# Activations or weights as the stationary operand: gates, outputs and feed-forward of one encoder block moved from "features by tokens" to "tokens by features"

## The chip, the cores and the metric

One core of a Trainium2 chip runs the whole block once. The metric is the device time of that run in microseconds (us). The kernel before took 1521.12 us (median of 3 runs, 1521.03 to 1523.44).

## What is computed

One layer on 256 tokens of width 2048, all in float32 (D = 2048, 16 heads of 128, feed-forward width 5632):

```python
h = rmsnorm(x, g_mix)
q_sb, k_sb, v_sb, q_ca, k_ca, v_ca, gate_sb, gate_ca = split(h @ w_in)     # 2048 x 10240
y_sb = stick_breaking_attention(q_sb, k_sb, v_sb)                           # 8 heads
y_ca = chunked_relpos_attention(q_ca, k_ca, v_ca, rel_bias)                 # 8 heads
merged = sigmoid(gate_sb) * (y_sb @ w_sb_out) + sigmoid(gate_ca) * (y_ca @ w_ca_out)
x = x + merged @ w_mix_out
g, u = split(rmsnorm(x, g_ffn) @ w_ffn_in)                                  # 2048 x 2*5632
x = x + (silu(g) * u) @ w_ffn_out
x = x + sigmoid(rmsnorm(x, g_ple) @ w_ple_gate) * (p @ w_ple_in)
out = rmsnorm(x, g_final)
```

## The kernel before

**Products.** Every large product is a list of *pieces*. A piece is one load of 512 KB of weights into a buffer `raw` (L147, queue of SP). ScalarE rounds it to `hi` (L176), VectorE takes the rest `lo = raw - hi` (L177), and TensorE multiplies (`products`, L188). The activations are kept in tables of the same two parts, features on the partitions: `T1`, `T2`, `T3`, each [128, 16, 2, 256] (feature tile, hi or lo, token). An exact enough float32 product is hi·hi + hi·lo + lo·hi.

There are two kinds of group (L129):

- `feat`: the **weights** are stationary. 256 output columns a group, four feature tiles a piece. For one feature tile and 128 output columns there is one matmul of 512 columns (`hi` with both parts of the table side by side, L201) and one of 256 (`lo` with the table's hi part, L203). The output is features by tokens, in two halves of a PSUM bank that `halves` (L231) adds up with one ScalarE copy and one VectorE add.
- `row`: the **activations** are stationary. 512 output columns a group, two feature tiles a piece, and for each feature tile and 128 tokens three matmuls of 512 columns (L184, L185, L186). The output is tokens by features, complete in one bank.

Before, the values of both attentions, `p @ w_ple_in` and the last product with `w_ple_gate` are `row`; all else is `feat`. So the residual is held as `xT`, features by tokens; `put_split` (L239) and `put_split_gain` (L243) make the next table straight from a group's output, and only the last stage turns `xT` back (`x2_chunk`, L668: 32 transposes).

**Norms.** The sums of squares are partial sums on GpSimd over the feature tiles (L93 to L97), finished by a matmul with ones (`nps`, L105); a further matmul (`rps`, L115) spreads the result over all partitions for `feat` groups (`rbc`).

**Order.** `flush` (L220) walks the pieces. Loads run five pieces ahead and the splitting two; a queue `tasks` gives attention steps and the like, run between pieces. A scheduler then sets each engine's final order from its own estimate of the times, so PE's order at the start is not that of the code.

**Stages, in order:** start (transposes of x, values of the first heads, `w_ple_in`), queries, keys, values and attention, gates, output products (`w_sb_out`, `w_ca_out`), `w_mix_out`, feed-forward in three blocks (16, 16 and 12 feature tiles wide), `w_ple_gate` with the final norm.

Of the kernel before, what the change touches and what calls it, by code (L numbers as in the profile page):

```python
# [16 lines left out]
P = 128  # L17
# [23 lines left out]
def block_kernel(ctx: ExitStack, tc: tile.TileContext, x, p, w_in, w_sb_out, w_ca_out, w_mix_out,  # L41
# [6 lines left out]

    nc = tc.nc
# [22 lines left out]
    const("fill", [P, 344])  # L72
# [18 lines left out]
    sqs = const("sqs", [P, 2, S])  # L91

    def square_sum(kt, sq):  # L93
        if kt == 0:
            nc.gpsimd.tensor_copy(sqs, sq)
        else:
            nc.gpsimd.tensor_tensor(sqs, sqs, sq, ALU.add)  # L97

    def norm(n):

        both = sqs[:, 0, :]
# [118 lines left out]
    def flush(every=1):  # L220

        while state["at"] < len(pieces):
# [16 lines left out]
    def put_split(dst, kt, src):  # L239
        nc.scalar.copy(dst[:, kt, 0, :], src)  # L240
        nc.vector.tensor_tensor(dst[:, kt, 1, :], src, dst.bitcast(F32)[:, kt, 0, :], ALU.subtract)

    def put_split_gain(dst, kt, src, gain):  # L243
        g = gT[:, gain + kt : gain + kt + 1]
        nc.scalar.activation(dst[:, kt, 0, :], src, AF.Identity, scale=g)
        nc.vector.scalar_tensor_tensor(dst[:, kt, 1, :], src, g, dst.bitcast(F32)[:, kt, 0, :],  # L246
                                       ALU.mult, ALU.subtract)
# [8 lines left out]
    xt = sp.tile([P, NT, D], F32, tag="xt", name="xt")  # L256
# [12 lines left out]
    def x_tiles(kt, ps):  # L269

        n = ps.shape[1]
        for k in range(n):
            for t in range(NT):
                nc.tensor.transpose(ps[:, k, t * P : (t + 1) * P], xt[:, t, (kt + k) * P : (kt + k + 1) * P], ident)
# [10 lines left out]
        nc.scalar.copy(xT[:, kt : kt + n, :], ps)  # L285

    def x_pair(kt):
# [5 lines left out]
        xk = xT[:, kt : kt + 2, :]  # L293
        sq = sp.tile([P, 2, S], F32, tag="sq", name="sq", bufs=2)
        nc.gpsimd.tensor_tensor(sq, xk, xk, ALU.mult)  # L295
        square_sum(kt, sq)
# [86 lines left out]
    gates = ap.tile([P, 2, KD, S], F32, tag="gates", name="gates", bufs=1)  # L383
# [172 lines left out]
    def gate_post(m, j):  # L556
        def post(ps):
            for f in range(2):
                sm = halves(ps[f], mp)
                nc.vector.tensor_tensor(gates[:, m, 2 * j + f, :], sm, rbc, ALU.mult)  # L560
        return post

    for j in range(8):
        for m in range(2):
            group("feat", w2, 6 * W + m * D + j * FB, range(KD), T1, gate_post(m, j), needs=hneed)
    flush(4)

    def out_post(m, j):
        def post(ps):
            gt = gates[:, m, 2 * j : 2 * j + 2, :]  # L570
            nc.scalar.activation(gt, gt, AF.Sigmoid)
            for f in range(2):
                kt = 2 * j + f
                sm = halves(ps[f], mp)
                nc.vector.tensor_tensor(gates[:, m, kt, :], sm, gates[:, m, kt, :], ALU.mult)
            if m == 1:
                for kt in (2 * j, 2 * j + 1):
                    mg = gates[:, 0, kt, :]
                    nc.gpsimd.tensor_tensor(mg, mg, gates[:, 1, kt, :], ALU.add)  # L579
                    put_split(T1, kt, mg)  # L580
        return post

    for j in range(8):
# [3 lines left out]
    flush(4)  # L587
    while tasks:
        run_task()
# [6 lines left out]
    x2 = lp.tile([P, NT, D], F32, tag="x2", name="x2")  # L596
    gf = lp.tile([P, D], F32, tag="gf", name="gf")
    dma_x.dma_start(gf, g_final.rearrange("(o d) -> o d", o=1).to_broadcast((P, D)))
    def norm_task(n):
        norm(n)  # L600
        if n == "ffn":
            tasks.append((None, lambda: broadcast_rstd(n, lp)))

    def residual_post(j, dst, gain, norm_of):

        def post(ps):
            for f in range(2):
                kt = 2 * j + f
                xk = xT[:, kt, :]
                nc.vector.tensor_tensor(xk, ps[f][:, :S], xk, ALU.add)  # L610
                nc.vector.tensor_tensor(xk, ps[f][:, S:], xk, ALU.add)  # L611
                if dst is not None:
                    put_split_gain(dst, kt, xk, gain)
            if dst is not None:
                sq = lp.tile([P, 2, S], F32, tag="tg", name="sq", bufs=2)
                nc.scalar.activation(sq, xT[:, 2 * j : 2 * j + 2, :], AF.Square)  # L616
                square_sum(2 * j, sq)
                if j == 7:
                    tasks.append((None, lambda: None))
                    tasks.append((None, lambda: norm_task(norm_of)))  # L620
        return post

    for j in range(8):
        group("feat", w_mix_out[0], j * FB, range(KD), T1, residual_post(j, T3, 16, "ffn"))
# [4 lines left out]
    def g_post(j):  # L629
        def post(ps):  # L630
            tg = lp.tile([P, 2, S], F32, tag="tg", name="tg", bufs=2)
            sg = lp.tile([P, 2, S], F32, tag="sg", name="sg", bufs=2)
            for f in range(2):
                sm = halves(ps[f], lp)
                nc.vector.tensor_tensor(tg[:, f, :], sm, rbc, ALU.mult)
            nc.scalar.activation(sg, tg, AF.Sigmoid)  # L636
            nc.gpsimd.tensor_tensor(tg, tg, sg, ALU.mult)  # L637
            hold[j] = tg
        return post

    def u_post(j, dst, kt0):
        def post(ps):
            tg = hold.pop(j)
            for f in range(2):
                sm = halves(ps[f], lp)
                nc.vector.tensor_tensor(sm, sm, rbc, ALU.mult)  # L646
                nc.vector.tensor_tensor(sm, sm, tg[:, f, :], ALU.mult)
                put_split(dst, kt0 + f, sm)
# [3 lines left out]
    for blk, nk in enumerate(FF_BLOCKS):  # L652
        dst = (T2, T1, T2)[blk]
        for i in range(0, nk, 2):
            j = (k0 + i) // 2
            group("feat", w_ffn_in[0], j * FB, range(KD), T3, g_post(j))
            group("feat", w_ffn_in[0], D_FF + j * FB, range(KD), T3, u_post(j, dst, i))
        last = blk == len(FF_BLOCKS) - 1
        for j in range(8):
            group("feat", w_ffn_out[0], j * FB, range(nk), dst,  # L660
                  residual_post(j, T1 if last else None, 32, "ple"), row0=k0)
# [6 lines left out]
    def x2_chunk(c):  # L668
        def fn():
            pi = pins[c] = lp.tile([P, NT, NB], F32, tag="pi", name="pi", bufs=2)  # L670
            dma_x.dma_start(pi, pin_d[:, :, c * NB : (c + 1) * NB])
            ps = aux("x2p")
            for t in range(NT):
                for k in range(4):
                    nc.tensor.transpose(ps[:, t * NB + k * P : t * NB + (k + 1) * P],  # L675
                                        xT[:, 4 * c + k, t * P : (t + 1) * P], ident)
            nc.scalar.copy(x2[:, :, c * NB : (c + 1) * NB], ps.rearrange("p (t n) -> p t n", t=2))
        return fn
# [5 lines left out]
    def gated(ps, t, c0, n, q):  # L684
# [3 lines left out]
        xc = x2[:, t, cs]  # L688
        sg = lp.tile([P, NB], F32, tag="sg", name="sgr", bufs=2)[:, :n]
# [3 lines left out]
        jk = lp.tile([P, NB], F32, tag="tg", name="jk", bufs=2)[:, :n]  # L693
# [3 lines left out]
    def with_gain(t, c0, n):  # L697
        xc = x2[:, t, c0 : c0 + n]
# [7 lines left out]
    def finish(t, q, n):  # L706
# [6 lines left out]
        for c in (0, 2, 1, 3):  # L713
            xc = x2[:, t, c * NB : (c + 1) * NB]
# [6 lines left out]
    def ple_post(c):  # L721
        def post(ps):
            for t in range(NT):
                gated(ps[t], t, c * NB, NB, c)
                with_gain(t, c * NB, NB)
        return post
# [48 lines left out]
```

## Time and profile before

| | |
|---|---|
| median of 3 runs | 1521.12 us |
| the profiled execution | 1521.23 us, span 1519.5 us |
| TensorE busy (PE) | 1502.3 us, 99% of the span |
| VectorE (DVE), ScalarE (ACT), GpSimd (POOL) busy | 991.9, 735.0, 129.6 us |
| DMA | 289.27 MB, 190 GB/s over the span |
| granted TensorE clock | 0.997 of full |

The rows further down are from the profiled execution. Start times count from the span's start. A matmul's duration in such a row runs from its start to its modelled end and overlaps the next one; what a matmul costs in a stream is the distance of two starts.

### The profile page before, as it was taken

What the parts mean: (1) busy time and instruction counts of PE and PEld (TensorE: products, weight loads), DVE (VectorE), ACT (ScalarE), POOL (GpSimd) and SP (SyncE); (2) the same over time, 40 slices, a digit from 0 to 9 for tenths busy, and PEclk for the clock granted to TensorE, in tenths of its full rate; (3) what the DMA queues carried; (4) which work ended last, traced back from release to release, by engine and by line L of the source; (5) the groups of instructions that cost most, each with busy time, mean ns of one, the idle gap of its engine ahead of it and who ended that gap; (6) DMA issues with size and microseconds to landing.
All of it is one profiled execution on the core that took longest, in us unless ns stands there. A gap on an engine that the chain in (4) does not pass through costs nothing.

```text
span 1519.5 us, 21785 instructions
## 1 busy us (share of the span) xinstructions
PE 1502.3 (99%) x8454; PEld 1303.0 (86%) x8454; DVE 991.9 (65%) x1361; ACT 735.0 (48%) x1001; POOL 129.6 (9%) x118
## 2 busy tenths in 40 slices
PE   8999999999999999999999999999999999999997
PEld 6888888888888888888888888888888888888886
DVE  7566666666555787676666655666665566668575
ACT  5455554555444555454444433444443344445542
POOL 6200000000000122111000000000000000001100
PEclk9999999999999999999999999999999999999999
DMA  7875656555566566656665655656656566555563
GB/s 268 258 222 167 173 173 179 182 174 173 182 192 185 189 195 211 220 181 186 187 191 184 194 188 187 193 183 191 188 187 194 186 188 192 184 184 192 176 213 120
DMA packets 265175, 289.27 MB, mean 190 GB/s; under 512 B 9041, under 2 KB 244865, under 8 KB 264817
## 3 DMA queue, kind: packets, MB, share of 16 engines
q1 hardware_dynamic: 262912, 278.96, 58.6%
q0 software_dynamic: 2160, 8.93, 1.8%
q8 instruction: 66, 1.08, 0.3%
q14 instruction: 37, 0.30, 0.1%
HBM read 282.09 MB, written 5.77 MB: 189 GB/s over the span
## 4 chain that ended last, share of the span: by engine, by line
PE 96%; POOL 1%; issue 1%; DVE 1%; DMA 0%; SPq 0%; ACT 0%; POOLq 0%; DVEq 0%
PE mm L201 56%; PE mm L203 28%; PE mm L184 3%; PE mm L185 3%; PE mm L186 3%; POOL sqs L97 1%; POOL sq L295 1%; DMA raw<-in_w_in 0%; DVE lo L177 0%; PE x2p L675 0%; PE yp L433 0%; PE wt L524 0%; PE zp L424 0%; PE zp L423 0%; PE zp L422 0%
## 5 line engine op out<-in xcount | busy, mean ns | idle before, releaser
L201 PE MATMUL mm<-T,hi 128*128 128x512 f32 x3648 | 1271.3, 396 | 0.0
L203 PE MATMUL mm<-T,lo 128*128 128x256 f32 x3648 | 1001.3, 279 | 0.0
L177 DVE TENSOR_TENSOR lo<-raw,hi 128x1024 fp32r<-128x1024 f32 (+1 forms) x517 | 641.3, 1241 | 410.5 <-ACT hi L176 404.8
L176 ACT CAST hi<-raw 128x1024 fp32r<-128x1024 f32 (+1 forms) x517 | 542.2, 1049 | 577.3 <-PE mm L201 435.2
L201 PEld LDWEIGHTS mm<-T,hi 128*128 128x128 f32 x3648 | 677.8, 188 | 154.4
L203 PEld LDWEIGHTS mm<-T,lo 128*128 128x128 f32 x3648 | 686.6, 188 | 8.7
L234 ACT COPY tm<-mm 128x256 f32<-128x256 f32 x184 | 68.6, 373 | 124.7 <-PE mm L203 124.7
L236 DVE TENSOR_TENSOR sm<-mm,tm 128x256 f32<-128x256 f32 x184 | 77.3, 420 | 53.0 <-ACT tm L234 53.0
L637 POOL TENSOR_TENSOR tg<-tg,sg 128x512 f32<-128x512 f32 x22 | 39.6, 1799 | 616.7 <-ACT sg L636 616.7
L185 PE MATMUL mm<-lo,T 128*128 128x512 f32 x224 | 87.9, 395 | 0.2 <-DVE lo L177 0.2
L186 PE MATMUL mm<-hi,T 128*128 128x512 f32 x224 | 86.7, 393 | 0.0
L184 PE MATMUL mm<-hi,T 128*128 128x512 f32 x224 | 83.0, 397 | 0.1
L185 PEld LDWEIGHTS mm<-lo,T 128*128 128x128 f32 x224 | 42.2, 189 | 9.0 <-DVE lo L177 0.6
L186 PEld LDWEIGHTS mm<-hi,T 128*128 128x128 f32 x224 | 42.1, 189 | 8.7
L184 PEld LDWEIGHTS mm<-hi,T 128*128 128x128 f32 x224 | 42.0, 189 | 8.6 <-ACT T L279 0.3
L579 POOL TENSOR_TENSOR gates<-gates 128x256 f32<-128x256 f32 x16 | 20.0, 1248 | 288.7 <-ACT hi L176 278.2
L97 POOL TENSOR_TENSOR sqs<-sqs,sq 128x512 f32<-128x512 f32 x21 | 30.8, 1468 | 117.6 <-ACT sq L616 117.3
L610 DVE TENSOR_TENSOR xT<-mm,xT 128x256 f32<-128x256 f32 x64 | 24.7, 424 | 10.4 <-PE mm L203 10.4
L246 DVE SCALAR_TENSOR_TENSOR T<-xT,gT,T 128x256 fp32r<-128x256 f32 x32 | 29.3, 956 | 0.0
L611 DVE TENSOR_TENSOR xT<-mm,xT 128x256 f32<-128x256 f32 x64 | 23.8, 414 | 0.0
L492 POOL DMA_DIRECT2D bias<-ext_d x8 | 4.3, 539 | 200.7 <-DVE sl L417 163.3
L646 DVE TENSOR_TENSOR sm<-sm,rbc 128x256 f32<-128x256 f32 x44 | 18.7, 425 | 1.5
(172 smaller groups left out, 626.7 us busy)
## 6 DMA issues: line engine op xcount, KB each, us to landing
raw<-in_w_ffn_in SPq DMA_DIRECT2D x176, 512.0 KB, 3.4
raw<-in_w_in SPq DMA_DIRECT2D x159, 512.0 KB, 3.5
raw<-in_w_ffn_out SPq DMA_DIRECT2D x88, 512.0 KB, 3.4
raw<-in_w_mix_out SPq DMA_DIRECT2D x32, 512.0 KB, 3.4
raw<-in_w_ple_gate SPq DMA_DIRECT2D x32, 512.0 KB, 4.5
raw<-in_w_sb_out SPq DMA_DIRECT2D x16, 512.0 KB, 3.4
raw<-in_w_ca_out SPq DMA_DIRECT2D x16, 512.0 KB, 3.5
raw<-in_w_ple_in SPq DMA_DIRECT2D x4, 512.0 KB, 4.8
```

The costliest lines, as they stand in the source:

```text
L97: nc.gpsimd.tensor_tensor(sqs, sqs, sq, ALU.add)
L176: nc.scalar.copy(hi[:, c : c + m], raw[:, c : c + m])
L177: nc.vector.tensor_tensor(lo[:, c : c + m], raw[:, c : c + m], hi.bitcast(F32)[:, c : c + m], ALU.subtract)
L184: nc.tensor.matmul(ps, xh, hi, start=a, stop=False)
L185: nc.tensor.matmul(ps, xh, lo, start=False, stop=False)
L186: nc.tensor.matmul(ps, xl, hi, start=False, stop=z)
L201: nc.tensor.matmul(ps, hi[:, i, f], lhs[:, kt, :, :].rearrange("p c s -> p (c s)"), start=a, stop=False)
L203: nc.tensor.matmul(ps[:, :S], lo[:, i, f], lhs[:, kt, 0, :], start=False, stop=z)
L234: nc.scalar.copy(tm, ps[:, S:])
L236: nc.vector.tensor_tensor(sm, ps[:, :S], tm, ALU.add)
L246: nc.vector.scalar_tensor_tensor(dst[:, kt, 1, :], src, g, dst.bitcast(F32)[:, kt, 0, :], ALU.mult, ALU.subtract)
L637: nc.gpsimd.tensor_tensor(tg, tg, sg, ALU.mult)
```

## The change

All products but queries and keys become `row` groups. The residual `x_` stays tokens by features, and whatever feeds a further product is turned by PE transposes in `into_table`: eight transposes of 128 x 128 for 512 features, then one split (or, with a gain, four) from PSUM into the table. `into_table` is put into `tasks` behind three empty tasks (`later`). The norms take their sums by ScalarE's Square with an accumulator. `x2_chunk` and the `nps` matmuls are gone.

```diff
-    xT = bp.tile([P, KD, S], F32, tag="xT", name="xT")
+    x_ = bp.tile([P, NT, D], F32, tag="x", name="x")
+    def square_sum(n, t, c, pool):
+        jk = pool.tile([P, NB], F32, tag="jk", name="jk", bufs=1)
+        nc.scalar.activation(jk, x_[:, t, c * NB : (c + 1) * NB], AF.Square, accum_out=sums[n][:, t, c : c + 1])
     def norm(n):
-        nc.gpsimd.tensor_tensor(both, both, sqs[:, 1, :], ALU.add)
-        ps = aux("nps")
-        for t in range(NT):
-            nc.tensor.matmul(ps[:, t : t + 1], both[:, t * P : (t + 1) * P], ones[:, 0:1], start=True, stop=True)
-        nc.vector.tensor_scalar(ms, ps[:, :NT], 1.0 / D, EPS, ALU.mult, ALU.add)
+        nc.vector.tensor_reduce(out=ms, in_=sums[n], op=ALU.add, axis=AX.X)
+        nc.vector.tensor_scalar(ms, ms, 1.0 / D, EPS, ALU.mult, ALU.add)
+    def later(fn, n=3):
+        for _ in range(n):
+            tasks.append((None, lambda: None))
+        tasks.append((None, fn))
+    def into_table(dst, c, src, gain=None, key=None):
+        ps = aux("tp").rearrange("p (k s) -> p k s", k=4)
+        for k in range(4):
+            for t in range(NT):
+                nc.tensor.transpose(ps[:, k, t * P : (t + 1) * P], src[:, t, k * P : (k + 1) * P], ident)
+        ks = slice(4 * c, 4 * c + 4)
+        if gain is None:
+            nc.scalar.copy(dst[:, ks, 0, :], ps)
+            nc.vector.tensor_tensor(dst[:, ks, 1, :], ps, dst.bitcast(F32)[:, ks, 0, :], ALU.subtract)
+        else:
+            for k in range(4):
...
+                nc.scalar.activation(dst[:, kt, 0, :], ps[:, k, :], AF.Identity, scale=g)
+                nc.vector.scalar_tensor_tensor(dst[:, kt, 1, :], ps[:, k, :], g, dst.bitcast(F32)[:, kt, 0, :],
+                                               ALU.mult, ALU.subtract)
-    for j in range(8):
+    for c in range(4):
         for m, wo in ((0, w_sb_out), (1, w_ca_out)):
-            group("feat", wo[0], j * FB, range(8 * m, 8 * m + 8), T2, out_post(m, j),
+            group("row", wo[0], c * NB, range(8 * m, 8 * m + 8), T2, out_post(m, c),
     def residual_post(c, key, gain):
         def post(ps):
+            for t in range(NT):
+                nc.vector.tensor_tensor(x_[:, t, cs], ps[t], x_[:, t, cs], ALU.add)
+            if key is not None:
+                for t in range(NT):
+                    square_sum(key, t, c, late["pool"])
+                later(lambda: into_table(dst, c, x_[:, :, cs], gain, key))
     def u_post(j, dst, c, key):
         def post(ps):
             for t in range(NT):
+                nc.vector.scalar_tensor_tensor(h[:, t, :], ps[t], r, tg[:, t, :], ALU.mult, ALU.mult)
+            later(lambda: into_table(dst, c, h, key=key))
+            group("row", w_ffn_in[0], j * NB, range(KD), T3, g_post(j), needs=fneed)
+            group("row", w_ffn_in[0], D_FF + j * NB, range(KD), T3, u_post(j, dst, c, key), needs=fneed)
```

**How the order moves.** First TensorE at the start. Before, the two `nps` matmuls of the first norm stand between the first and the second group of `p @ w_ple_in` (mm_404 and mm_441):

```order
L186 MATMUL mm0_404<-hi_380,pT_107 128x512
L184 MATMUL mm1_405<-hi_380,pT_107 128x512
L185 MATMUL mm1_405<-lo_381,pT_107 128x512
L186 MATMUL mm1_405<-hi_380,pT_107 128x512
L105 MATMUL nps_419<-ones_79,sqs_90 128x1 x2
L184 MATMUL mm0_441<-hi_396,pT_107 128x512
L185 MATMUL mm0_441<-lo_397,pT_107 128x512
```

Now there is no such matmul; the one left of the norm (`rps`) stands in the first group of values (mm0_167, mm1_168), 14 large matmuls before that group's end:

```order
L182 MATMUL mm1_168<-lo_311,T1_71 128x512
L312 MATMUL pps_357<-ident_74,pt_103 128x128
L112 MATMUL rps_409<-dg_406,ones_79 128x256
L183 MATMUL mm0_167<-hi_310,T1_71 128x512
L183 MATMUL mm1_168<-hi_310,T1_71 128x512
```

What TensorE waits for at the start is thus another chain, and it stands earlier in its order.

Then TensorE in the feed-forward. Before, no row stood here between two products. Now the eight transposes of a hidden tile (`h_5876`, the product of the group mm_5736) stand inside the next group (mm_5885), the first four behind 26 of its matmuls and the others ten matmuls later:

```order
L181 MATMUL mm0_5885<-hi_5881,T3_4951 128x512
L181 MATMUL mm1_5886<-hi_5881,T3_4951 128x512
L247 MATMUL tp_5935<-ident_74,h_5876 128x128 x4
L182 MATMUL mm0_5885<-lo_5882,T3_4951 128x512
L183 MATMUL mm0_5885<-hi_5881,T3_4951 128x512
```

And VectorE at the same place. Before, at the end of a `u` group, each half of 256 tokens took an add and two products from `sm`, and the split into the table:

```order
L236 TENSOR_TENSOR sm_6647<-mm0_6561,tm_6645 128x256
L646 TENSOR_TENSOR sm_6647<-sm_6647,rbc_86 128x256
L177 TENSOR_TENSOR lo_6664<-raw_6579,hi_6663 128x1024
L647 TENSOR_TENSOR sm_6647<-sm_6647,tg_6541 128x256
L236 TENSOR_TENSOR sm_6655<-mm1_6562,tm_6653 128x256
```

Now there are two products of 512 columns straight from PSUM, four splits of weights, and then the table's lo part from the transposed tile:

```order
L646 SCALAR_TENSOR_TENSOR h_5876<-mm0_5736,rstd_ffn_88,tg_5725 128x512
L646 SCALAR_TENSOR_TENSOR h_5876<-mm1_5737,rstd_ffn_88,tg_5725 128x512
L174 TENSOR_TENSOR lo_5882<-raw_5822,hi_5881 128x1024
L174 TENSOR_TENSOR lo_5902<-raw_5840,hi_5901 128x1024
L174 TENSOR_TENSOR lo_5920<-raw_5858,hi_5919 128x1024
L174 TENSOR_TENSOR lo_5949<-raw_5879,hi_5948 128x1024
L251 TENSOR_TENSOR T2_72<-tp_5935,T2_72 128x4x256
```

The way from a product to its table now crosses TensorE once more, between VectorE's two steps.

## Rows read from the trace of the kernel before

**Rows 1.** Page, busy us, share of the span and instructions of each engine
```profile
PE 1502.3 (99%) x8454; PEld 1303.0 (86%) x8454; DVE 991.9 (65%) x1361; ACT 735.0 (48%) x1001; POOL 129.6 (9%) x118
```
**Rows 2.** Chain that ended last, shares of the span by engine, tile and line
```profile
by line: PE mm L201 55.9%; PE mm L203 28.1%; PE mm L184 3.4%; PE mm L185 3.3%; PE mm L186 3.3%; issue 0.8%; POOL sqs L97 0.7%; POOL sq L295 0.6%; DMA raw<-in_w_in 0.5%; DVE lo L177 0.2%; PE x2p L675 0.2%; PE yp L433 0.2%; PE wt L524 0.2%; P
```
**Rows 3.** Costliest groups: line, engine, op, out<-in, count | busy us, mean ns
```profile
L201 PE MATMUL mm<-T,hi 128*128 128x512 f32 x3648 | 1271.3, 396 | 0.0
```
**Rows 4.** Chain in order of time, w_ple_gate stage: start us, us, what
```profile
1444.48 0.45 PE mm L184 x2
...
1477.12 0.45 PE mm L184 x2
```
**Rows 5.** Timeline of PE, w_ple_gate stage: start us, us, engine, line, op
```profile
1427.17 0.50 PE L105 MATMUL nps<-ones,sqs 128*128 128x1 f32 x4
1427.53 1.07 PE L675 MATMUL x2p<-ident,xT 128*128 128x128 f32 x8
...
1431.43 0.39 PE L184 MATMUL mm<-hi,T 128*128 128x512 f32 x1
1431.66 1.03 PE L675 MATMUL x2p<-ident,xT 128*128 128x128 f32 x8
1432.45 0.48 PE L185 MATMUL mm<-lo,T 128*128 128x512 f32 x1
```
**Rows 6.** Timeline of PE at the start
```profile
37.26 0.39 PE L186 MATMUL mm<-hi,pT 128*128 128x512 f32 x1
40.11 0.61 PE L105 MATMUL nps<-ones,sqs 128*128 128x1 f32 x4 [2.46 <-POOL sqs L102]
...
43.28 0.63 PE L184 MATMUL mm<-hi,pT 128*128 128x512 f32 x1
43.70 0.53 PE L185 MATMUL mm<-lo,pT 128*128 128x512 f32 x1
...
45.00 0.59 PE L115 MATMUL rps<-dg,ones 128*128 128x256 f32 x2
...
45.70 0.50 PE L184 MATMUL mm<-hi,pT 128*128 128x512 f32 x1
...
51.29 0.39 PE L201 MATMUL mm<-T,hi 128*128 128x512 f32 x1
```
**Rows 7.** Timeline of POOL at the start
```profile
8.55 1.12 POOL L295 TENSOR_TENSOR sq<-xT 128x512 f32<-128x512 f32 x1 [4.88 <-ACT xT L285]
...
40.99 0.73 POOL L108 TENSOR_TENSOR rstd_mix<-ms_mix,mhalf 128x2 f32<-128x2 f32 x1 [0.94 <-DVE ms_mix L107]
```
**Rows 8.** Timeline of ACT at the start
```profile
22.61 1.06 ACT L176 CAST hi<-raw 128x1024 fp32r<-128x1024 f32 x1 [1.43 <-PE mm L186]
```
**Rows 9.** Timeline of DVE at the start
```profile
28.46 2.22 DVE L177 TENSOR_TENSOR lo<-raw,hi 128x1024 fp32r<-128x1024 f32 x1
```
**Rows 10.** Groups by form, one instruction's price: PE, ACT, DVE
```profile
L675 PE MATMUL x2p<-ident,xT 128*128 128x128 f32 x32 | 4.2, 273 | 0.0
L677 ACT COPY x<-x2p 128x1024 f32<-128x1024 f32 x4 | 4.1, 1013 | 1.7 <-PE x2p L675 1.7
L616 ACT ACTIVATE sq<-xT 128x512 f32<-128x512 f32 x16 | 9.9, 617 | 0.0
L511 ACT ACTIVATION_READ_ACCUMULATOR zs<-zs,mx 128x1 f32 x16 | 3.0, 188 | 0.0
L692 DVE TENSOR_TENSOR x<-x,sgr 128x512 f32<-128x512 f32 x7 | 4.6, 686 | 0.0
L177 DVE TENSOR_TENSOR lo<-raw,hi 128x1024 fp32r<-128x1024 f32 x515 | 639.9, 1243 | 409.7 <-ACT hi L176 403.9
L236 DVE TENSOR_TENSOR sm<-mm,tm 128x256 f32<-128x256 f32 x184 | 77.3, 420 | 53.0 <-ACT tm L234 53.0
```
**Rows 11.** Timeline of PE, first matmuls of the w_ple_gate stage
```profile
1418.48 0.40 PE L184 MATMUL mm<-hi,T 128*128 128x512 f32 x1
...
1421.04 0.39 PE L186 MATMUL mm<-hi,T 128*128 128x512 f32 x1
```

More of the change, by code (lines that the diff above doesn't have):

```diff
@@ L90, in block_kernel @@
     rstd = {n: const(f"rstd_{n}", [P, NT]) for n in ("mix", "ffn", "ple")}
[L91 to L97, printed above, removed]
-    def norm(n):
-        both = sqs[:, 0, :]
-        nc.gpsimd.tensor_tensor(both, both, sqs[:, 1, :], ALU.add)
-        ps = aux("nps")
-        for t in range(NT):
-            nc.tensor.matmul(ps[:, t : t + 1], both[:, t * P : (t + 1) * P], ones[:, 0:1], start=True, stop=True)
+    sums = {n: const(f"sum_{n}", [P, NT, 4]) for n in ("mix", "ffn", "ple")}
+    def square_sum(n, t, c, pool):
+        jk = pool.tile([P, NB], F32, tag="jk", name="jk", bufs=1)
+        nc.scalar.activation(jk, x_[:, t, c * NB : (c + 1) * NB], AF.Square, accum_out=sums[n][:, t, c : c + 1])
+    def norm(n):
         ms = const(f"ms_{n}", [P, NT])
-        nc.vector.tensor_scalar(ms, ps[:, :NT], 1.0 / D, EPS, ALU.mult, ALU.add)
+        nc.vector.tensor_reduce(out=ms, in_=sums[n], op=ALU.add, axis=AX.X)
+        nc.vector.tensor_scalar(ms, ms, 1.0 / D, EPS, ALU.mult, ALU.add)
         return nc.gpsimd.tensor_tensor(rstd[n], ms, mhalf, ALU.pow)
@@ L218, in prefetch, with flush @@
             state["split"] += 1
-    def flush(every=1):
-        while state["at"] < len(pieces):
+    def later(fn, n=3):
+        for _ in range(n):
+            tasks.append((None, lambda: None))
+        tasks.append((None, fn))
+    def flush(every=1, until=None):
+        while state["at"] < len(pieces) and (until is None or until not in done):
             pc = pieces[state["at"]]
@@ L237, in halves @@
         return sm
[L239 to L247, printed above, removed]
+    def into_table(dst, c, src, gain=None, key=None):
[9 more added lines that the diff above has]
+            for k in range(4):
+                kt = 4 * c + k
+                g = gT[:, gain + kt : gain + kt + 1]
+                nc.scalar.activation(dst[:, kt, 0, :], ps[:, k, :], AF.Identity, scale=g)
+                nc.vector.scalar_tensor_tensor(dst[:, kt, 1, :], ps[:, k, :], g, dst.bitcast(F32)[:, kt, 0, :],
+                                               ALU.mult, ALU.subtract)
+        for k in range(4):
+            done.add((key, 4 * c + k))
     mid_stack = ExitStack()
@@ L273, in x_tiles @@
             for t in range(NT):
-                nc.tensor.transpose(ps[:, k, t * P : (t + 1) * P], xt[:, t, (kt + k) * P : (kt + k + 1) * P], ident)
+                nc.tensor.transpose(ps[:, k, t * P : (t + 1) * P], x_[:, t, (kt + k) * P : (kt + k + 1) * P], ident)
         for k in range(n):
@@ L292, in x_pair @@
             x_tiles(kt, aux("xps").rearrange("p (k n) -> p k n", k=2))
[L293 to L296, printed above, removed]
+        if kt % 4 == 2:
+            for t in range(NT):
+                square_sum("mix", t, kt // 4, sp)
     def p_transposes():
@@ L381, in block_kernel @@
         dma_x.dma_start(ext_d, ext)
-    gates = ap.tile([P, 2, KD, S], F32, tag="gates", name="gates", bufs=1)
+    gates = ap.tile([P, NT, 2, D], F32, tag="gates", name="gates", bufs=1)
     def feat_post(dst, h0, sc, then):
@@ L554, in block_kernel, with gate_post @@
             flush(4)
-    def gate_post(m, j):
+    def gate_post(m, c):
         def post(ps):
-            for f in range(2):
-                sm = halves(ps[f], mp)
-                nc.vector.tensor_tensor(gates[:, m, 2 * j + f, :], sm, rbc, ALU.mult)
+            for t in range(NT):
+                nc.scalar.activation(gates[:, t, m, c * NB : (c + 1) * NB], ps[t], AF.Identity,
+                                     scale=rstd["mix"][:, t : t + 1])
         return post
-    for j in range(8):
+    for c in range(4):
@@ L564, in block_kernel, with out_post @@
         for m in range(2):
-            group("feat", w2, 6 * W + m * D + j * FB, range(KD), T1, gate_post(m, j), needs=hneed)
+            group("row", w2, 6 * W + m * D + c * NB, range(KD), T1, gate_post(m, c), needs=hneed)
     flush(4)
-    def out_post(m, j):
+    def out_post(m, c):
         def post(ps):
-            gt = gates[:, m, 2 * j : 2 * j + 2, :]
+            cs = slice(c * NB, (c + 1) * NB)
+            gt = gates[:, :, m, cs]
             nc.scalar.activation(gt, gt, AF.Sigmoid)
[L572 to L575, printed above, removed]
+            for t in range(NT):
+                nc.vector.tensor_tensor(gates[:, t, m, cs], ps[t], gates[:, t, m, cs], ALU.mult)
@@ L576, in post @@
             if m == 1:
[L577 to L580, printed above, removed]
+                mg = gates[:, :, 0, cs]
+                nc.vector.tensor_tensor(mg, mg, gt, ALU.add)
+                later(lambda: into_table(T1, c, mg, key="mg"))
         return post
-    for j in range(8):
+    for c in range(4):
         for m, wo in ((0, w_sb_out), (1, w_ca_out)):
-            group("feat", wo[0], j * FB, range(8 * m, 8 * m + 8), T2, out_post(m, j),
+            group("row", wo[0], c * NB, range(8 * m, 8 * m + 8), T2, out_post(m, c),
@@ L586, in block_kernel, with residual_post, post @@
                   needs=lambda kt: ("y", kt))
-    flush(4)
-    while tasks:
-        run_task()
+    flush()
+    late = {}
+    def residual_post(c, key, gain):
+        def post(ps):
+            cs = slice(c * NB, (c + 1) * NB)
+            for t in range(NT):
+                nc.vector.tensor_tensor(x_[:, t, cs], ps[t], x_[:, t, cs], ALU.add)
+            if key is not None:
+                for t in range(NT):
+                    square_sum(key, t, c, late["pool"])
+                if c == 3:
+                    norm(key)
+                dst = T1 if key == "ple" else late["T3"]
+                later(lambda: into_table(dst, c, x_[:, :, cs], gain, key))
+        return post
@@ L590, in block_kernel @@
+    for c in range(4):
+        group("row", w_mix_out[0], c * NB, range(KD), T1, residual_post(c, "ffn", 16), needs=lambda kt: ("mg", kt))
+    flush(until=("mg", KD - 1))
     att.close()
@@ L595, in block_kernel @@
     T3 = lp.tile([P, KD, 2, S], F32R, tag="T3", name="T3")
-    x2 = lp.tile([P, NT, D], F32, tag="x2", name="x2")
+    late.update(pool=lp, T3=T3)
     gf = lp.tile([P, D], F32, tag="gf", name="gf")
     dma_x.dma_start(gf, g_final.rearrange("(o d) -> o d", o=1).to_broadcast((P, D)))
[L599 to L624, printed above, removed]
     flush()
@@ L630, in post, with u_post @@
         def post(ps):
[L631 to L638, printed above, removed]
+            sg = lp.tile([P, NT, NB], F32, tag="sg", name="sg")
+            tg = hold[j] = lp.tile([P, NT, NB], F32, tag="tg", name="tg")
+            for t in range(NT):
+                r = rstd["ffn"][:, t : t + 1]
+                nc.scalar.activation(sg[:, t, :], ps[t], AF.Sigmoid, scale=r)
+                nc.vector.scalar_tensor_tensor(tg[:, t, :], ps[t], r, sg[:, t, :], ALU.mult, ALU.mult)
         return post
-    def u_post(j, dst, kt0):
+    def u_post(j, dst, c, key):
         def post(ps):
             tg = hold.pop(j)
[L644 to L648, printed above, removed]
+            h = lp.tile([P, NT, NB], F32, tag="h", name="h", bufs=2)
+            for t in range(NT):
+                r = rstd["ffn"][:, t : t + 1]
+                nc.vector.scalar_tensor_tensor(h[:, t, :], ps[t], r, tg[:, t, :], ALU.mult, ALU.mult)
+            later(lambda: into_table(dst, c, h, key=key))
         return post
@@ L652, in block_kernel @@
     for blk, nk in enumerate(FF_BLOCKS):
[L653 to L657, printed above, removed]
+        dst, key = (T2, T1, T2)[blk], f"h{blk}"
+        for c in range(nk // 4):
+            j = k0 // 4 + c
+            fneed = lambda kt: ("ffn", kt)
+            group("row", w_ffn_in[0], j * NB, range(KD), T3, g_post(j), needs=fneed)
+            group("row", w_ffn_in[0], D_FF + j * NB, range(KD), T3, u_post(j, dst, c, key), needs=fneed)
         last = blk == len(FF_BLOCKS) - 1
-        for j in range(8):
-            group("feat", w_ffn_out[0], j * FB, range(nk), dst,
-                  residual_post(j, T1 if last else None, 32, "ple"), row0=k0)
+        for c in range(4):
+            group("row", w_ffn_out[0], c * NB, range(nk), dst, residual_post(c, "ple" if last else None, 32),
+                  needs=lambda kt, key=key: (key, kt), row0=k0)
         k0 += nk
@@ L666, in block_kernel, with pin_load @@
     pins = {}
[L668 to L678, printed above, removed]
+    def pin_load(c):
+        pi = pins[c] = lp.tile([P, NT, NB], F32, tag="h", name="pi", bufs=2)
+        dma_x.dma_start(pi, pin_d[:, :, c * NB : (c + 1) * NB])
     msq = const("msq", [P, NT, 5])
@@ L687, in gated @@
         pi = pins[c0 // NB][:, t, c0 % NB : c0 % NB + n]
-        xc = x2[:, t, cs]
-        sg = lp.tile([P, NB], F32, tag="sg", name="sgr", bufs=2)[:, :n]
+        xc = x_[:, t, cs]
+        sg = lp.tile([P, NB], F32, tag="sgr", name="sgr", bufs=2)[:, :n]
         nc.scalar.activation(sg, ps, AF.Sigmoid, scale=rstd["ple"][:, t : t + 1])
@@ L692, in gated @@
         nc.vector.tensor_tensor(xc, xc, sg, ALU.add)
-        jk = lp.tile([P, NB], F32, tag="tg", name="jk", bufs=2)[:, :n]
+        jk = lp.tile([P, NB], F32, tag="jk", name="jk")[:, :n]
         nc.vector.scalar_tensor_tensor(jk, xc, 1.0 / D, xc, ALU.mult, ALU.mult,
@@ L745, in last_post @@
         finish(1, 4, FB)
-    for c in range(4):
-        tasks.append((None, x2_chunk(c)))
+    pin_load(0)
+    pin_load(1)
+    pneed = lambda kt: ("ple", kt)
     for c in range(3):
-        group("row", w_ple_gate[0], c * NB, range(KD), T1, ple_post(c))
-    group("row", w_ple_gate[0], 3 * NB, range(KD), T1, last_post, keep=keep)
+        group("row", w_ple_gate[0], c * NB, range(KD), T1, ple_post(c), needs=pneed)
+    group("row", w_ple_gate[0], 3 * NB, range(KD), T1, last_post, needs=pneed, keep=keep)
     flush()
```

12 lines of the change are left out of this document (6 added, 6 removed).

## The prediction

> **What bounds the kernel now.** I read the busy times first. TensorE is busy for 99% of the span, VectorE 65%, ScalarE 48%, GpSimd 9% [rows 1]. A busy TensorE says little by itself, since a matmul's duration overlaps the next one, so the chain of waits came second. There the reader should see that nearly all of it is matmuls: the two of the `feat` products hold 55.9% and 28.1% of the span, the three of the `row` products ten per cent together, and nothing else holds one per cent except the GpSimd sums of squares, 0.7% and 0.6% [rows 2]. TensorE thus works in a stream almost without gaps, and a change is worth what it takes from that stream or opens in it. Third I took the distance of two starts in the stream, as the price of a matmul in either kind of product. Fourth, I looked at the one place where TensorE waits, the first norm.
>
> **Term 1, the products.** The chain gives the `feat` pair (512 + 256 columns) its price: 84.0% of 1519.5 us is 1276.4 us, over 3648 pairs [rows 2, 3], so 349.9 ns a pair, whatever disturbs it included. For the `row` product the w_ple_gate stage shows it: from 1444.48 to 1477.12 us lie twelve pieces of twelve matmuls [rows 4], 32.64 us over 144, so 226.7 ns each.
> Count in units of one feature tile by 512 output columns. A unit is four pairs as `feat`, 1399.6 ns, or six matmuls as `row`, 1360.0 ns. Both stream 3072 columns; the `row` unit has two instructions fewer. What moves: gates 8 x 16 units, output products 8 x 8, w_mix_out 4 x 16, the feed-forward's first product 22 x 16, its second 4 x 44; together 784 units, or 3136 of the 3648 pairs (the other 512 are queries and keys). 784 x 39.6 ns = **-31.0 us**. Bounds: if the `row` stream is as disturbed as the `feat` stream on average (its undisturbed pair, 512 + 256 columns with the same 13 ns over 2.4 columns a ns on each matmul, would take 346.7, so 0.9% more), 4704 matmuls cost 9.6 us more and -21 is left; if it ran throughout like the first matmuls of the w_ple_gate stage, which start 2.56 us / 11 = 232.7 ns apart [rows 11], 28.2 us more and -3 is left. I take 226.7, since 144 matmuls in a row show it and 12 the other.
>
> **Term 2, the transposes.** `into_table` is called 4 times for the merged values, 4 for the feed-forward's input, 11 for hidden tiles, 4 for the last stage: 23 batches of 8, 184 transposes. The 32 of `x2_chunk` go. A batch of eight is in the trace: a matmul starts at 1431.43, the batch follows, the next matmul starts at 1432.45 [rows 5]; less one matmul, eight take 0.79 us, 99 ns each. 184 x 99 = +18.2 us, 32 x 99 = -3.2 us: **+15.0 us**. Split into four and four, as now, a batch might cost a little more at its second border; I have no row for that and put it into the range, bounded by one matmul distance a batch, 5 us.
> The row of the group shows 273 ns for one such transpose [rows 10]; by the starts, they overlap, and the price is 99. The Trainium skill's page "TensorE: Matmul & The Clock Gate", Part 4, speaks against the change here: it puts a 128 x 128 transpose at about 275 ns inside a kernel. The trace has that number as a duration and not as a distance; with 275 as the price term 2 would be near +47 us, which is the first rival below.
>
> **Term 3, the norms' matmuls.** `nps` of the two later norms: four small matmuls, 0.36 us from start to start of what follows [rows 5], twice; `rps` of the second norm, two in about 0.4 us, from the 0.70 us that it and the small `gps` take at the start [rows 6]. **-1.1 us**.
>
> **Term 4, the start.** GpSimd squares and sums the sixteen feature tiles from 8.55 us on, and the norm's last step ends near 41.7 [rows 7]. TensorE has nothing but `nps` to do next in its order: it stands after the matmul of 37.26 and gets to `nps` at 40.11, and the following matmuls start 0.42 us apart instead of 0.227 [rows 6]. Without this, the 36 matmuls of `p @ w_ple_in` that are left would end 36 x 0.227 + 0.70 = 8.9 us after 37.49, at 46.4; the first queries start at 51.29. So 4.9 us are at stake.
> Now ScalarE squares each 512 features by itself, straight from the loaded x: eight times 617 + 188 = 0.81 us [rows 10]. They stand between its other work; the last two stand behind the split that before began at 22.61 [rows 8] and one table write, so they end near 26. VectorE's sum over four numbers, GpSimd's power (0.73 us [rows 7]) and VectorE's diagonal follow: near 28.5. TensorE comes to `rps`, behind 82 matmuls of the first group, at about 31. So it finds it ready, with two us to spare. What it costs: VectorE's sum stands in its queue ahead of two table writes and a split of weights, and waits up to 1.5 us for ScalarE; TensorE may lose half a us to a later split. On the other hand VectorE's split took 2.22 us while GpSimd worked [rows 9], 1.24 on average [rows 10], and GpSimd is idle now. I take **-4.4 us**, bounds 0 (another wait takes the place) and -5.5.
>
> **What is hidden.** VectorE and ScalarE lose work: of 184 adds of halves at 420 ns [rows 10], 152 go, with as many ScalarE copies, and the products that followed on halves become ones of 512 columns at 686. New are 23 table writes, about 2.3 us of both engines. Their cover is the 21.8 us of a group of 96 matmuls. TensorE reaches the transposes 26 matmuls, 5.9 us, after the group that feeds them. The longest way to a ready source is that of the merged values: a split in front (1.24), two products (0.69 each), an add of 1024 (1.24), 3.9 us. After that a table write takes 1.0 us on ScalarE and 1.24 on VectorE, and its first reader stands at least 24 matmuls behind the transposes, 5.4 us. Nothing is late by this; behind a late batch the whole stream would wait, since TensorE keeps its order. I allow **+1.5 us** for a place or two, where a queue is fuller than I count.
>
> **The sum.** -31.0 + 15.0 - 1.1 - 4.4 + 1.5 = -20.0. The profiled execution took 1521.23 us, span 1519.5 and 1.7 around it, and agrees with the median of 1521.12, so the forecast is **1501 us**.
>
> **Rivals.** *Exposed transposes (slower).* If a batch does not pipeline, since its source has just been written and each transpose costs its duration of 273 ns, the 184 cost 50.2 instead of 18.2: 1501 + 32 = 1533. The place is all 23 batches; it decides from 0.87 us a batch over the price above (20 / 23). For: the duration. Against: the eight of the last stage, whose distance was 99 with a source long written, and the starts of x's transposes, which no long gap follows. 3%.
> *The saving per unit is not there (slower).* `row` matmuls at 232.7 all along: 1501 + 28 = 1529. For: the stretch above, in which all of VectorE, GpSimd and the loads were at work. Against: the 144 after it, with splits and loads at the same pace. 5%. The same page of the Trainium skill, "Back-to-back issue gap", gives columns / 2.4 + 2.5 ns for a matmul in a stream; by it the unit would fall from 1300 to 1295 ns and term 1 to -4 us, so the time to about 1528. This trace disagrees: 226.7 instead of 215.8.
> *A new wait at the tables.* Each batch late by 1 us: 1501 + 23 - 1.5 = 1522, no change; by 0.3 us, 1506. For: the stream has no slack of its own. Against: two us in the worst way above, and lighter queues. 4% for 0.9 us or more, 10% for something like a third.
> *The start does not heal:* 1501 + 4.4 = 1505. 13%.
> The forecast itself, with its smaller errors, 65%.
>
> **How the numbers follow.** About 0.2%, 3 us, is what a measurement of this kernel can tell from none. The forecast, the healed start's failure and the smaller waits all are faster: 88%. No change, 4%, is the full wait at the tables; slower, 8%, the first two. The range: below, a start that heals in full and no waits, 1498, and a stream of 226.0, 1495; above, the disturbed stream (+10) or borders of the batches and an unhealed start: 1512.
>
> **What would show it.** In the profile after: the L105 row of TensorE gone and no wait of over 1 us in its first 60 us; the first queries near 47 us; starts of `row` matmuls 227 ns apart in the feed-forward; eight transposes in 0.8 us; TensorE's idle time under 5 us between 50 and 1480. A gap of TensorE ahead of transposes, or one ahead of the first product that reads a new table, would make it wrong; so would a stream at 232 ns.

## The result and the profile after

The changed kernel takes **1504.1 us** (median, 1504.01 to 1504.34, 4 runs) against 1521.07 for the kernel before: 0.9887 of the time, interval [0.987, 0.9904], so 17 us faster. Run again beside the last experiments it took 1504.1 again, 0.9894 [0.9879, 0.9909]. The forecast was 1501, the range 1495 to 1512.

The profiled execution has a span of 1502.4 us. The first line of its page answers to [rows 1], the shares of the chain by line to [rows 2]:

```profile
PE 1488.2 (99%) x7024; PEld 1243.8 (83%) x7024; DVE 851.3 (57%) x936; ACT 700.8 (47%) x831; POOL 24.1 (2%) x45
```

```profile
by line: PE mm L183 27.6%; PE mm L181 27.6%; PE mm L182 27.6%; PE mm L198 8.0%; PE mm L200 4.0%; PE tp L247 1.3%; issue 0.7%; DMA x<-in_x 0.4%; PE xps L286 0.2%; PE yp L443 0.2%; PE wt L534 0.2%; PE zp L434 0.1%; PE zp L433 0.1%; PE zp L432
```

The program is still one stream of matmuls, now mostly the three of the `row` product (L181 to L183); the `feat` pair is down to 8% and 4%. The transposes (L247) hold 1.3%, 20 us, and the GpSimd sums have left the chain. VectorE has lost 141 us of work, which could buy little by itself: before, TensorE had waited 0.2 us for it in the whole run.

What TensorE waited for in the whole run (engine, line, what it waited for, us, times, longest) is two loads in its first 6 us:

```profile
PE gps L278 <- DMA gm<-in_g_mix: 3.4, 1, 3.4
PE xps L286 <- DMA x<-in_x: 1.8, 1, 1.8
```

So no transposes and no table made it wait. At the start, TensorE's timeline (start us, us, engine, line, operation), in answer to [rows 6], and VectorE's:

```profile
31.71 0.60 PE L112 MATMUL rps<-dg,ones 128*128 128x256 f32 x2
...
46.59 0.39 PE L198 MATMUL mm<-T,hi 128*128 128x512 f32 x1
```

```profile
23.22 0.15 DVE L103 TENSOR_REDUCE ms_mix<-sum_mix 128x2 f32<-128x8 f32 x1
...
25.73 0.47 DVE L110 TENSOR_SCALAR dg<-ident,rstd_mix 128x128 f32<-128x128 f32 x2
```

The diagonal that `rps` needs is written by 26.2 us, more than five before TensorE comes to it, and the first queries start at 46.59 instead of 51.29.

The chain in order of time gives the periods, in answer to [rows 4]. First the output products (two groups of 48 matmuls and one batch of eight transposes), then the feed-forward's second product (eight pieces without a batch), then its first (two groups of 96 and one batch, split in two):

```profile
518.59 0.46 PE mm L181 x2
...
541.25 0.46 PE mm L181 x2
...
721.95 0.46 PE mm L181 x2
...
766.46 0.46 PE mm L181 x2
...
833.71 0.45 PE mm L181 x2
...
855.47 0.46 PE mm L181 x2
```

Without a batch, 96 matmuls take 21.76 us, 226.7 ns each, what the prediction took from before. A whole batch costs 22.66 - 21.76 = 0.90 us, a split one 44.51 - 43.52 = 0.99 us. The prediction had 0.79. The timeline at such a half batch, in answer to [rows 5], shows what it left out:

```profile
724.77 0.40 PE L183 MATMUL mm<-hi,T 128*128 128x512 f32 x1
725.01 0.60 PE L247 MATMUL tp<-ident,h 128*128 128x128 f32 x4
725.36 0.48 PE L181 MATMUL mm<-hi,T 128*128 128x512 f32 x1
725.68 0.40 PE L182 MATMUL mm<-lo,T 128*128 128x512 f32 x1
725.91 0.40 PE L183 MATMUL mm<-hi,T 128*128 128x512 f32 x1
...
727.76 0.39 PE L182 MATMUL mm<-lo,T 128*128 128x512 f32 x1
727.99 0.39 PE L183 MATMUL mm<-hi,T 128*128 128x512 f32 x1
```

Four transposes take 0.35 us; but then the first matmul behind them holds its successor back by 0.32 instead of 0.227 us, and the next nine start (727.76 - 725.68) / 9 = 231 ns apart. The same delay stood in the trace before, one row below the last of [rows 5]:

```profile
1432.45 0.48 PE L185 MATMUL mm<-lo,T 128*128 128x512 f32 x1
1432.77 0.39 PE L186 MATMUL mm<-hi,T 128*128 128x512 f32 x1
```

### The profile page after: what moved, and what is told of

The parts are those of the page before. It is cut to its first block, busy times and chain, and to the rows that moved or that the text cites. A ratio compares the mean times of both kernels' runs of the same rounds, so it can differ in the third digit from the quotient of the medians.

```text
span 1502.4 us, 18130 instructions
## 1 busy us (share of the span) xinstructions
PE 1488.2 (99%) x7024; PEld 1243.8 (83%) x7024; DVE 851.3 (57%) x936; ACT 700.8 (47%) x831; POOL 24.1 (2%) x45
## 4 chain that ended last, share of the span: by engine, by line
PE 98%; issue 1%; DMA 0%; DVE 0%; SPq 0%; POOL 0%; POOLq 0%; ACT 0%; DVEq 0%
PE mm L183 28%; PE mm L181 28%; PE mm L182 28%; PE mm L198 8%; PE mm L200 4%; PE tp L247 1%; DMA x<-in_x 0%; PE xps L286 0%; PE yp L443 0%; PE wt L534 0%; PE zp L434 0%; PE zp L433 0%; PE zp L432 0%; PE yp L434 0%; PE yp L432 0%
## 5 line engine op out<-in xcount | busy, mean ns | idle before, releaser
L182 PE MATMUL mm<-lo,T 128*128 128x512 f32 x1792 | 700.4, 391 | 0.0
L183 PE MATMUL mm<-hi,T 128*128 128x512 f32 x1792 | 697.6, 390 | 0.0
L181 PE MATMUL mm<-hi,T 128*128 128x512 f32 x1792 | 640.2, 392 | 0.0
L183 PEld LDWEIGHTS mm<-hi,T 128*128 128x128 f32 x1792 | 336.7, 188 | 69.4
L182 PEld LDWEIGHTS mm<-lo,T 128*128 128x128 f32 x1792 | 337.0, 188 | 68.6
L181 PEld LDWEIGHTS mm<-hi,T 128*128 128x128 f32 x1792 | 336.7, 188 | 68.8
L198 PE MATMUL mm<-T,hi 128*128 128x512 f32 x512 | 180.3, 398 | 0.0
L200 PE MATMUL mm<-T,lo 128*128 128x256 f32 x512 | 140.8, 280 | 0.0
L198 PEld LDWEIGHTS mm<-T,hi 128*128 128x128 f32 x512 | 95.3, 188 | 21.5
L200 PEld LDWEIGHTS mm<-T,lo 128*128 128x128 f32 x512 | 96.3, 189 | 1.2
L237 ACT COPY tm<-mm 128x256 f32<-128x256 f32 x32 | 11.9, 373 | 24.2 <-PE mm L200 24.2
L239 DVE TENSOR_TENSOR sm<-mm,tm 128x256 f32<-128x256 f32 x32 | 13.5, 421 | 10.4 <-ACT tm L237 10.4
```

Source lines behind the costliest of these rows:

```text
L181: nc.tensor.matmul(ps, xh, hi, start=a, stop=False)
L182: nc.tensor.matmul(ps, xh, lo, start=False, stop=False)
L183: nc.tensor.matmul(ps, xl, hi, start=False, stop=z)
L198: nc.tensor.matmul(ps, hi[:, i, f], lhs[:, kt, :, :].rearrange("p c s -> p (c s)"), start=a, stop=False)
L200: nc.tensor.matmul(ps[:, :S], lo[:, i, f], lhs[:, kt, 0, :], start=False, stop=z)
```

## The experiments

The theory: the time goes down by the two instructions fewer of each unit (term 1) and by the healed start (term 4), and the transposes take most of term 1 back, at a batch price of 0.9 to 1.0 us and without any wait. Its rivals: the transposes cost what the prediction said or their durations; the gain is only the disturbed pairs of before; the start gained by something else.

**Transposes left out** (`e1_no_transposes`).

```diff
-                nc.tensor.transpose(ps[:, k, t * P : (t + 1) * P], src[:, t, k * P : (k + 1) * P], ident)
+        sv = src.rearrange("p t (j n) -> p t j n", j=2)
...
-            nc.scalar.copy(dst[:, ks, 0, :], ps)
...
+                nc.scalar.copy(dst[:, kk, 0, :], sv[:, t])
...
```

> The changed kernel with the 184 transposes left out: each table is written from the untransposed tile, so the values are in the wrong places. If a batch of eight really costs 0.97 us (from the period of two groups and a batch, 44.51 us, less 192 x 0.2267, and 0.90 where the batch is unsplit), 23 of them are 22 us: 1504.1 - 22 = 1482. If a batch costs 0.79 us, as the prediction had it, 1504.1 - 18 = 1486. If the transposes cost their durations (273 ns each, 50 us), 1454.

Measured: 1481.56 us (1481.02 to 1481.9), 0.9746 [0.9731, 0.976] of before. That is 22.5 us less than the changed kernel, 0.98 us a batch. The changed kernel was timed beside other runs than this one; the kernel before took 1521.07 and 1520.64 there and 1520.43 here, so 22.5 and the 20.0 of the next run are known to about 0.6 us. The 23 batches take back what they were measured to cost by the periods, and the prediction's 0.79 (18 us) is out.

**Transposes doubled** (`e2_double_transposes`).

```diff
-        for k in range(4):
-            for t in range(NT):
-                nc.tensor.transpose(ps[:, k, t * P : (t + 1) * P], src[:, t, k * P : (k + 1) * P], ident)
+        for _ in range(2):
+            for k in range(4):
+                for t in range(NT):
+                    nc.tensor.transpose(ps[:, k, t * P : (t + 1) * P], src[:, t, k * P : (k + 1) * P], ident)
```

> The changed kernel with every batch of eight transposes done twice in a row into the same tile. The second eight have no border of their own. If one costs 0.107 us in a row (0.79 for eight, 0.35 for four), +23 x 8 x 0.107 = +19.7: 1524. If they are priced at 0.099 each, 1522. If a transpose costs its duration of 273 ns, 1554.

Measured: 1524.07 us (1523.88 to 1524.69), 1.0027 [1.0017, 1.0037] of before: slower than before the change, and 20.0 us above the changed kernel, so 0.109 us for each further transpose in a row. Their duration of 273 ns would have given 50 us. With the run without: the eight alone are 0.87 us, and 0.11 of the 0.98 are borders, to which doubling adds little (TensorE's order has 45 stretches of transposes instead of 41).

**The new norm at the start alone** (`e3_start_norm`), put into the kernel before:

```diff
-        nc.gpsimd.tensor_tensor(sq, xk, xk, ALU.mult)
-        square_sum(kt, sq)
+        if kt % 4 == 2:
+            c = kt // 4
+            for t in range(NT):
...
+                nc.scalar.activation(jk, xt[:, t, c * NB : (c + 1) * NB], AF.Square, accum_out=smix[:, t, c : c + 1])
...
-        started["norm"] = norm("mix")
...
+        nc.vector.tensor_reduce(out=ms, in_=smix, op=ALU.add, axis=AX.X)
...
```

> The kernel before with one part of the change: the first norm's sums by ScalarE's Square from the loaded x, no nps matmul at the start; all else as before. If the wait for GpSimd's sums was the whole loss at the start, the first queries start near 46.6 us instead of 51.3 and the time is 1521.1 - 4.7 = 1516.4. If the healed start needs the dropped copies of x as well (ScalarE keeps them here, 4.8 us), it gains 2 to 4. If the start gained by something else in the change, 1521.

Measured: 1516.39 us (1516.0 to 1516.76), 0.9974 [0.9964, 0.9983]: 4.0 us less than before on that chip (interval 2.6 to 5.5). TensorE's timeline has

```profile
32.85 0.59 PE L115 MATMUL rps<-dg,ones 128*128 128x256 f32 x2
...
46.38 0.39 PE L201 MATMUL mm<-T,hi 128*128 128x512 f32 x1
```

The queries start 4.9 us earlier, though ScalarE still makes the copies of x. The wait for GpSimd's sums, with what came behind it, was the loss. It had two parts. TensorE stood from 37.49 to 40.11, 2.6 us [rows 6]. Then it ran at the lower of its two clock levels, 1.2 instead of 2.4 GHz: these are its timeline before, and the window from 42 to 44 us (stretch, length, busy us of PE, PEld, DVE, ACT and POOL, granted clock, DMA share, GB/s), first before and then in this experiment.

```profile
40.57 0.77 PE L184 MATMUL mm<-hi,pT 128*128 128x512 f32 x1
...
44.07 0.39 PE L186 MATMUL mm<-hi,pT 128*128 128x512 f32 x1
```

```profile
42.00:44.00 2.00, 2.00 (x6) 1.61 (x5) 1.37 (x3) 1.50 (x3) 0.38 (x1) 0.50 0.55 226
```

```profile
42.00:44.00 2.00, 2.00 (x11) 1.65 (x10) 1.23 (x1) 1.04 (x2) 0.70 (x1) 1.00 0.86 235
```

From 40.57 to 44.07 eight matmuls took 3.50 us, where eight at 226.7 ns take 1.81. Without the wait the clock stays at 1.00, here and in the changed kernel.

Between this kernel and the one without transposes lie terms 1 and 3 and the removed `x2_chunk`: 1516.39 - 1481.56 = 34.8 us.

**Term 1 by itself** (`e5_ffn_in_row`): in the kernel before, only the feed-forward's first product as `row`.

```diff
-            group("feat", w_ffn_in[0], j * FB, range(KD), T3, g_post(j))
-            group("feat", w_ffn_in[0], D_FF + j * FB, range(KD), T3, u_post(j, dst, i))
...
+            group("row", w_ffn_in[0], j * NB, range(KD), T3, g_post(j))
+            group("row", w_ffn_in[0], D_FF + j * NB, range(KD), T3, u_post(j, dst, c))
```

> The kernel before with only the first product of the feed-forward (352 of the 784 units) as row groups; the hidden tiles go into the table untransposed, so the values are in the wrong places, and there are no transposes. If a unit is worth 39.6 ns, -13.9: 1507. If a matmul cost only 2.5 ns beside its columns, a unit would be worth 5 ns, -1.8: 1519. If the gain is nothing but the disturbed pairs' (349.9 against 346.7), 352 x 4 x 3.2 ns = -4.5: 1516.6.

Measured: 1509.81 us (1508.7 to 1510.48), 0.9931 [0.9916, 0.9946]: 10.6 us less than before on that chip (1520.43), between the first expectation and the last. The chain of this kernel, from the first `row` groups of block 0 to the second product of block 1:

```profile
700.21 0.45 PE mm L184 x2
...
852.53 0.45 PE mm L184 x2
855.25 0.45 PE mm L201 x2
...
1119.76 0.45 PE mm L201 x2
```

The `row` pieces stand 2.72 us apart (152.32 us over 56), so the unit costs the 1360 ns that it should. Of the 264.51 us from one second product to the next, eight `row` groups take 174.08; 90.43 are left for 256 `feat` pairs, 353.2 ns each. In the kernel before, a period of the same 24 groups, all `feat`, is:

```profile
708.88 0.46 PE mm L201 x2
...
976.81 0.47 PE mm L201 x2
```

267.93 us. And its second product ran faster. The chain gives the pace there by the distance of starts, first 170 pairs of the kernel before, then 195 of the experiment:

```profile
881.62 0.23 PE mm L201
...
940.55 0.23 PE mm L201
```

```profile
870.01 0.23 PE mm L201
...
938.91 0.23 PE mm L201
```

That is 346.7 against 353.3 ns a pair; the granted clock is 1.00 in both stretches. At 346.7 the 256 pairs of the second product take 88.8 us. So the first product gained 267.93 - 88.8 - 174.08 = 5.1 us a block of 128 units, 39 to 40 ns a unit, and the untouched second product lost 1.7, because its pairs ran at a slower pace. The size of term 1 is confirmed; that the pace of a pair differs by place was not expected.

The kernel before shows how the pace changes. In its feed-forward the two paces take turns, and the turn comes at nearly every place where two hi matmuls (L201) stand side by side, here at 742.39 and again at 753.68:

```profile
734.76 0.23 PE mm L201
...
742.04 0.23 PE mm L201
...
742.39 0.46 PE mm L201 x2
...
743.80 0.23 PE mm L201
...
753.34 0.23 PE mm L201
...
753.68 0.47 PE mm L201 x2
```

The 21 pairs before 742.04 take 346.7 ns each and the 27 before 753.34 take 353.3; about half of each makes the mean near 349.9 from which the prediction worked.

**Batches unsplit** (`e4_later2`):

```diff
-    def later(fn, n=3):
+    def later(fn, n=2):
```

> The changed kernel with two empty tasks ahead of a table's transposes instead of three. The eight transposes of a batch then stand in one piece in TensorE's order everywhere, 24 to 26 matmuls behind their group, where before 18 or 19 of 23 batches stood as four and four or five and three. If each border costs a late matmul and some slow ones behind it (0.98 us for a split batch, 0.90 for an unsplit one), -1.5: 1502.6. If the border is free and 0.98 has another cause, 1504. If a batch now comes before its source, TensorE waits, and the time goes above 1505.

The changed kernel beside it:

> The changed kernel once more, on the chip of the next three, so that differences of one or two us can be read: 1504.1.

Measured: 1502.32 us (1502.29 to 1502.82) beside 1504.1 (1503.89 to 1504.37) of the changed kernel on the same chip: 1.8 us less, the two sets of times do not overlap. TensorE's timeline:

```profile
721.10 0.39 PE L183 MATMUL mm<-hi,T 128*128 128x512 f32 x1
721.33 1.03 PE L247 MATMUL tp<-ident,h 128*128 128x128 f32 x8
722.12 0.48 PE L181 MATMUL mm<-hi,T 128*128 128x512 f32 x1
722.43 0.40 PE L182 MATMUL mm<-lo,T 128*128 128x512 f32 x1
722.66 0.39 PE L183 MATMUL mm<-hi,T 128*128 128x512 f32 x1
722.90 0.39 PE L181 MATMUL mm<-hi,T 128*128 128x512 f32 x1
723.12 0.39 PE L182 MATMUL mm<-lo,T 128*128 128x512 f32 x1
```

1.33 us less two matmuls is 0.88 for a batch and its border. There is one border instead of two, and behind it the stream is back at its pace after two slow matmuls, where behind a half batch there were nine.

**The order inside a pair** (`e6_order` on top of the one before, `e7_before_order` on the kernel before), since the pace of pairs changed where two hi matmuls stood side by side. For one feature tile the order was hi, lo, hi, lo; now it is hi, hi, lo, lo:

```diff
-                    nc.tensor.matmul(ps, hi[:, i, f], lhs[:, kt, :, :].rearrange("p c s -> p (c s)"),
-                                     start=a, stop=False)
-                    nc.tensor.matmul(ps[:, :S], lo[:, i, f], lhs[:, kt, 0, :], start=False, stop=z)
...
+                for t in range(2):
+                    nc.tensor.matmul(g["ps"][t], hi[:, i, t * P : (t + 1) * P],
+                                     lhs[:, kt, :, :].rearrange("p c s -> p (c s)"), start=a, stop=False)
+                for t in range(2):
+                    nc.tensor.matmul(g["ps"][t][:, :S], lo[:, i, t * P : (t + 1) * P], lhs[:, kt, 0, :],
+                                     start=False, stop=z)
```

> The one before (two empty tasks) with the 512 pairs left of feat in another order: both hi matmuls of a feature tile, then both lo ones. If this order sets the pace of a pair (345.5 or 353 ns were both seen, and the pace changed at such places), 512 pairs gain 1.7 us at most or lose 1.6; if not, no change against the one before.

> The kernel before with all 3648 pairs in that order. If the order holds the pace at 345.5 to 346.7 ns throughout, -12 to -16 us: 1505 to 1509, and much of what the change gained in term 1 was to be had without it. If it holds the slow pace of 353, +11: 1532. If the pace has nothing to do with the order, 1520.4.

Measured: the first 1501.01 us (1500.89 to 1501.66), 1.3 less than the one before and **the fastest kernel here that computes the whole layer**, 0.9875 [0.9858, 0.9891] of before. The second 1516.11 us (1514.31 to 1518.03), 0.997 [0.9959, 0.9982]: 4.5 us less than before, none of the three expectations. (The faster pace, put at 345.5 in the first expectation, is 346.7 by the starts.) Its chain:

```profile
712.25 0.47 PE mm L200 x2
713.65 0.47 PE mm L200 x2
...
804.21 0.47 PE mm L200 x2
805.61 0.47 PE mm L200 x2
```

From 712.25 to 805.61 lie 67 feature tiles of two pairs each, so 1.393 us a tile and 696.7 ns for two pairs: 348.4 ns a pair, a third pace, and here it takes no turns. That is 1.5 ns below the mean of 349.9, 5.5 us over 3648 pairs; 4.5 were measured.

## Why the prediction was right, and where its sizes were off

The forecast's mechanism held: a gain from fewer instructions and from the start, most of it spent on transposes, no new wait. By its steps:

- **Term 1**, -31.0. Confirmed: the feed-forward's first product alone gained 39 to 40 ns a unit, and `row` matmuls at 226.7 ns in the feed-forward are in the trace. The 34.8 us between the start-norm kernel and the one without transposes fit: less the four batches of `x2_chunk` at 0.88 (3.5) and term 3 as predicted (1.1), 30.2 are left, though as a remainder. But the prediction's reason covers only a part of it. Against the faster of the two paces a unit saves 4 x 346.7 - 1360 = 26.8 ns, the two instructions fewer, or 21 us over 784 units. The other 10 us came from what kept the pairs above 346.7 on average, above all the slower pace. The prediction counted that as disturbance and did not know what it was, so that nearly all of it went away was luck; its bound of -21 is the other case.
- **Term 2**, +15.0. This is the term that was mis-sized. "Eight take 0.79 us, 99 ns each" was read between two neighbouring starts, and a batch's price goes on past the next matmul: 0.98 us by the run without transposes, so +22.5, less 3.5 for the removed ones at the same kind of price, +19.0. The split into four and four, put into the range at up to 5 us, accounts for 1.8 of the four missing; the rest is the delay behind a whole batch, 0.90 instead of 0.79.
- **Term 3**, -1.1: too small to be tested alone, so not shown.
- **Term 4**, -4.4. The queries start 4.7 us earlier, and the part alone gives 4.0 (2.6 to 5.5). The prediction had the 0.42 us between starts behind the wait, but not its cause, the clock at 0.50: a wait of 2.6 us cost 1.7 more after it had ended. The diagonal was ready at 26.2 instead of 28.5. ScalarE's last two squares stand ahead of the split and not behind it, as the prediction had them, and end at 22.3 instead of 26; the power on GpSimd took 1.56 us instead of 0.73.
- **The allowance for waits**, +1.5: none came. TensorE's list of waits has no entry after the first 6 us. The unused 1.5 hid a part of what term 2 lacked.
- By the measured sizes the sum is -30.2 + 19.0 - 1.1 - 4.0 = -16.3, against 17.0 measured. This is no test of the terms: it is made of the differences between the same runs and adds up whatever the terms are. The 0.7 left over is the kernel before, 1521.07 beside the changed kernel and 1520.43 beside the experiments. What stands by itself is the unit's price in one product, a batch's price by periods, by leaving out and by doubling, and the start put into the kernel before.

Of the rivals, exposed transposes are out by the doubled ones (0.109 us each against 0.273). So the about 275 ns on the Trainium skill's page "TensorE: Matmul & The Clock Gate", Part 4, is a duration here and no price. The missing saving per unit is out by the feed-forward's `row` pace. The prediction took columns / 2.4 + 2.5 ns as the price of a matmul in a stream. The same page of the Trainium skill gives it for matmuls back to back in the section "Wait — 56ns, not 53.3ns?", but the section that the prediction named, "Back-to-back issue gap", calls it the gap of an isolated matmul. The trace decides: 226.7 ns and not 215.8. Still, a slow pace like the rival's is real: about 231 ns for nine matmuls behind each half batch of transposes, and it is part of a batch's price.

## What to carry to other kernels

Price an inserted instruction over a whole period with it and without it, not between its neighbours: here the batch cost a quarter more than the gap that it opened. A product with the activations stationary is only a little cheaper per column (two of eight instructions, 13 ns each, make 27 of the 40 ns a unit here), so it pays where few transposes are needed: doubling them ate the whole gain. Before changing the layout, look whether the old stream has two paces: another order of the same instructions gave 4.5 us without it. And look for the one place where a saturated engine waits, and for its clock behind the wait: one norm's chain was worth a quarter of the total here.

## What the runs showed of the hardware

- A `feat` pair of 512 and 256 columns runs at one of several steady paces with the granted clock at 1.00 and no wait in the trace: 346.7 and 353.3 ns in the order hi, lo, hi, lo, and 348.4 in the order hi, hi, lo, lo. In the first order the pace changes in the feed-forward at nearly every place where two hi matmuls stand side by side. What sets it stays open; the order of the instructions has a part in it, as the last two runs show.
- Transposes of 128 x 128 in a row cost 0.109 us each, not their durations of 0.27. The stream behind them starts 0.09 us late and runs at 231 instead of 226.7 ns for nine matmuls behind a stretch of four transposes, and for two behind a stretch of eight.
- Behind a wait of 2.6 us TensorE's granted clock was 0.50, the level of 1.2 GHz, and eight matmuls of 512 columns took 3.50 instead of 1.81 us.
